# Decoder layer on one core: the feed-forward stage and the end go through the same instruction recorder as the stages before

## The chip, the cores and the metric

The kernel runs on one core of a Trainium2 chip. That core has five instruction streams: TensorE (PE) for matmuls, VectorE (DVE), ScalarE (ACT) and GpSimd (POOL) for elementwise work, and SyncE (SP), which here only issues DMA transfers. Each stream runs its instructions in the order in which the program has them; a semaphore wait holds up everything behind it in the same stream. The metric is the device time in microseconds (us) of one execution.

## The reference

One layer of a decoder is computed in float32 for a prompt of 512 tokens and for 8 samples of 4 tokens each, 544 token columns in all, with shared weights (1024 model channels, 2816 feed-forward channels):

```python
h = rmsnorm(x, norm_mix)
z = h @ w_in                       # dilated attention: q, k, v; HGRN2: q, f, i, gate
att = dilated_attention(...)       # three (window, dilation) patterns, 8 heads of 64
o, s_new = hgrn2_recurrence(...)   # 4 heads, 128 x 128 state, chunks
x = x + concatenate([att, o]) @ w_out
cq = rmsnorm(x, norm_cross) @ w_cq
co = softmax(cq @ mem_k.T * X_DH ** -0.5) @ mem_v     # 4 heads, 256 memory rows
x = x + co @ w_co
u = rmsnorm(x, norm_ffn)
ug = u @ w_gate
up = concatenate([conv_buf, ug])   # two earlier rows
conv = conv_b + sum(conv_w[j] * up[:, j:j + T] for j in range(3))
x = x + (silu(conv) * (u @ w_up)) @ w_down
y = rmsnorm(x, norm_final)
```

Outputs are y for prompt and samples, the new keys and values, the memory's keys and values, the HGRN2 states and the last two gate rows of the convolution.

## The kernel before

Activations lie transposed, channels on partitions and the 544 tokens along the free axis. Every float32 operand of a large product is split in two parts, `h` (a cast to the PE's reduced float format, on ACT) and `l` (the rest, a subtraction on DVE), and a product is made of three passes, `h*h`, `l*h` and `h*l`. The tokens are cut in two halves: columns 0 to 256 and 256 to 544 (`CUTS`), and for the last product 0 to 288 and 288 to 544 (`LAST_CUTS`). A product of one output tile (128 channels) and one half goes to one PSUM tile: tag `dense` with two buffers, tag `aux` with five.

**Two planners.** The stages up to the end of the cross attention are *told* to a recorder, the class `Tape`. Its engine objects (`_Engine`) do not issue; they record each instruction as a part of a `Step`, with the tiles it reads and writes. Steps told inside `tape.main()` keep the order in which they are told (the backbone of dense products); all others are side steps. `Tape.due` works back from the backbone to a due time (`begin`) for each step. `Tape.plan` then runs an event loop: on each engine, of the side steps that are ready and due within `LEAD` = 15 us, the one with the earliest due time goes next, if its buffers are free (`fits`). Side steps of PE go in bursts between main ones. A step may also be held by a gate: it isn't told to run before a certain main step (`AHEAD` counts how many main steps back that lies). All this runs in three rounds, and then the calls are issued in the order found.

The feed-forward stage has another planner, `Plan`, with `Job`s whose lengths are written by hand. A `Job` for PE keeps its place; the rest gets a due time from its users and an optional `lead` before which it isn't begun. An evacuation of PSUM has `within`, a due time counted from the end of its product. The end of the kernel is written out without a planner: `ffn_last`, `last_by_half` and `last_half` issue products, with lists `evacs` and `pending` that hold back the work on the results by one step, and `sides` pumps one generator step (`conv_last`, `final`) after each product.

**The feed-forward stage.** 22 gate tiles and 22 up tiles (`ug`, `up`) of 128 channels. Tiles 0 to 3 are plain: 24 matmuls for each half (`ps_g0_0`, `ps_g0_256`, `ps_u0_0` and so on). Tiles 4 to 21 go in pairs by a Strassen-Winograd scheme of seven products: 2 x 2 blocks over (channel tile, token half) and model channels. It needs sums of weight blocks (up to signs): `S1` of A21 and A22 and `S3` of A11 and A21, which come by a plain load through SP followed by an accumulating load through POOL's software queue (`load_sum`), and `S2` of S1 and A11 and `S4` of S2 and A12 on DVE, and sums of activation blocks `X, T, U, V` (`combine`), each split in `h` and `l` again. A name like `S1u10` is the sum S1 for the pair of up tiles 10 and 11. On the finished gate tile ACT, DVE and ACT make the convolution and silu (`cv`); POOL copies its last rows out (`last<-ug`), multiplies `up` by `cv` for the prompt (`up<-up,cv`), and ACT and DVE split the result to `h3h`, `h3l` and so on (one pair for each tile). Down products of four tiles at a time (`ps_d0_m` for tiles 0 to 3 and output tile m, then `d4`, `d8`, `d12`, `d16` for two tiles) stand between the pairs' products, and are added to the residual `xr` by DVE.

**The end.** The last four tiles (18 to 21) go down as `ps_dz`, first half for all eight output tiles, then the second half. Squares of the final residual are summed on POOL (`acc_final`), the column sums are made by PE (`psr_final`), ACT makes the reciprocal root by a logarithm and an exponential (`r_fin`), for which a table has to be loaded, and DVE and POOL scale the result (`y`). The first half's `final(0)` is pumped while the second half's products run.

Large SBUF tiles of one size share a tag `a` with 59 buffers. In `Tape.plan` such a tile is given out early only if 12 (`SPARE`) stay free, unless it is due within 8 us (`SOON`).

Of the kernel before, what the change touches and what calls it, by code (L numbers as in the profile page):

```python
# [16 lines left out]
D = 1024  # L17
# [153 lines left out]
class Job:  # L171


    def __init__(self, engine, length, fn, deps, lead=None, within=None, takes=None, gives=None):
        self.engine, self.length, self.fn, self.lead = engine, length, fn, lead
        self.within, self.takes, self.gives = within, takes, gives
        self.deps, self.users = [d for d in deps if d is not None], []
        for d in self.deps:
            d.users.append(self)


class Plan:

    STEP = 0.1

    def __init__(self, **banks):
        self.jobs, self.order, self.banks = [], [], {tag: [0.0] * n for tag, n in banks.items()}

    def add(self, engine, length, fn, *deps, **more):

        self.jobs.append(Job(engine, length, fn, deps, **more))
        return self.jobs[-1]

    def pe(self, length, fn, *deps, takes=None):
        self.order.append(self.add("PE", length, fn, *deps, takes=takes))
        return self.order[-1]

    def run(self):

        t = 0.0  # L200
        for i, j in enumerate(self.order):
            j.place, j.begin = i, t
            t += j.length
        late = t + 100.0
        for j in reversed(self.jobs):
            if j.engine != "PE":
                j.begin = min([u.begin for u in j.users] + [late]) - j.length - self.STEP
                if j.within is not None:
                    j.begin = min(j.begin, max(d.begin + d.length for d in j.deps if d.engine == "PE") + j.within)
        for i, j in enumerate(self.jobs):  # L210
            j.waits, j.number = len(j.deps), i
            j.ready = 0.0 if j.lead is None else max(0.0, j.begin - j.lead)
        free, done = {}, []
        waiting = [j for j in self.jobs if not j.waits]
        left, now, place = len(self.jobs), 0.0, 0
        while left:
            best, soonest = None, None
            for j in waiting:
                if j.engine == "PE" and j.place != place:
                    continue  # L220
                if j.takes and not self.banks[j.takes]:
                    continue
                start = max(j.ready, now, 0.0 if j.engine == "SP" else free.get(j.engine, 0.0),
                            min(self.banks[j.takes]) if j.takes else 0.0)
                soonest = start if soonest is None else min(soonest, start)
                if start <= now + 1e-9 and (best is None or (j.begin, j.number) < (best.begin, best.number)):
                    best = j
            if best is None:
                assert soonest is not None
                now = soonest  # L230
                continue
            waiting.remove(best)
            left -= 1
            best.start, best.end = now, now + best.length
            if best.engine == "PE":
                place += 1
            free[best.engine] = best.end
            if best.takes:
                self.banks[best.takes].remove(min(self.banks[best.takes]))
            if best.gives:  # L240
                self.banks[best.gives].append(best.end + self.STEP)
# [2011 lines left out]
```

## Time and profile before

| | us |
|---|---|
| median of 3 executions | 839.62 (839.14 to 839.94) |
| profiled execution | 839.75 |
| its span in the trace | 838.0 |
| PE busy | 821.8 (98%) |
| DVE busy | 590.5 (70%) |
| ACT busy | 396.4 (47%) |
| POOL busy | 180.1 (21%) |
| mean granted PE clock | 0.996 |

The span is counted from the first to the last instruction of the trace; 1.75 us of the execution lie around it. Stages by time: mixing (norm, projections, attention, HGRN2, `w_out`) to about 370, cross attention to about 452, plain feed-forward tiles to about 503, pairs of tiles and down products to about 804, the last product and the final norm to 838. In the windows view a row has the window, its length, then for each of PE, PE weight loads, DVE, ACT and POOL the busy time and the number of instructions, then the granted PE clock, the busy share of the DMA engines and GB/s. In the list of waits a row has the engine, the operation that waited, what ended the wait, and the us in total, the number of times and the longest. In the timeline a row has start and duration, and in brackets how long the engine was idle before it and what ended that. In the list of groups a row ends with the busy time, the mean ns of one, and the idle time before them. In the list of transfers the last number is the median time in us from issue to landing.

### The profile page before, as it was taken

The numbers are of one execution on the slowest core, as the hardware profiler recorded it, in microseconds if no ns is written. First come the engines' busy times: TensorE is split into PE (matmuls) and PEld (weight loads), VectorE is DVE, ScalarE is ACT, GpSimd is POOL, SyncE is SP. The second block draws the span as 40 slices with busy tenths as digits, with TensorE's granted clock in tenths as the row PEclk, the third lists the DMA queues.
The fourth block names the chain that finished last, engine by engine and source line by source line (L and its number), as shares of the span: only waits on it lengthen the run. The fifth ranks groups of instructions, "written<-read, shape, count | busy, mean of one in ns | idle before, by whom it ended". The sixth has DMA issues, their size and how long they took to land.

```text
span 838.0 us, 18847 instructions
## 1 busy us (share of the span) xinstructions
PE 821.8 (98%) x7594; PEld 767.3 (92%) x7594; DVE 590.5 (70%) x1233; ACT 396.4 (47%) x792; POOL 180.1 (21%) x261
## 2 busy tenths in 40 slices
PE   9999999999999999999999999999999999999996
PEld 8988888778889879998889999999999999999995
DVE  6684735865888986564556899878777776777764
ACT  7412424443545644343545456465454554544633
POOL 1140000210120220222233232324213222322113
PEclk9999999999999999999999999999999999999999
DMA  9566787866842635260621237656544654564403
GB/s 320 203 188 185 235 264 239 293 203 201 282 141 85 200 89 160 75 223 27 222 91 51 81 92 184 157 144 171 144 128 127 153 161 122 145 154 114 136 23 108
DMA packets 90760, 132.33 MB, mean 158 GB/s; under 512 B 6064, under 2 KB 60080, under 8 KB 90544
## 3 DMA queue, kind: packets, MB, share of 16 engines
q1 hardware_dynamic: 84480, 120.69, 44.8%
q0 software_dynamic: 5184, 9.44, 6.9%
q8 instruction: 60, 0.98, 0.5%
q10 hardware_dynamic: 1008, 0.99, 0.4%
q14 instruction: 28, 0.23, 0.1%
HBM read 123.03 MB, written 8.07 MB: 156 GB/s over the span
## 4 chain that ended last, share of the span: by engine, by line
PE 88%; DVE 6%; issue 2%; DMA 2%; ACT 1%; POOL 0%; SPq 0%; DVEq 0%; POOLq 0%; ACTq 0%
PE ps_d L797 12%; PE ps_ag L2039 6%; PE ps_au L2039 6%; PE ps_wo L593 6%; PE ps_co L593 3%; PE ps_cg L2039 3%; PE ps_k L593 3%; PE ps_q L593 3%; PE ps_cq L593 3%; PE ps_hv L593 3%; PE ps_cu L2039 3%; PE ps_g L797 2%; PE ps_hq L593 2%; PE ps_hf L593 2%; PE ps_hg L593 2%; PE ps_dz L797 2%
## 5 line engine op out<-in xcount | busy, mean ns | idle before, releaser
L593 ACT CAST wh<-wr 128x1024 fp32r<-128x1024 f32 (+1 forms) x61 | 53.3, 892 | 109.7 <-PE ps_q L593 20.0
L593 DVE TENSOR_TENSOR wl<-wr,wh 128x1024 fp32r<-128x1024 f32 (+1 forms) x61 | 65.4, 1080 | 9.7 <-ACT wh L593 9.3
L593 POOL TENSOR_TENSOR hG<-hG,hf 128x256 f32<-128x256 f32 (+1 forms) x28 | 25.8, 921 | 192.2 <-DVE hf L593 142.2
L1809 POOL TENSOR_TENSOR up<-up,cv 128x512 f32<-128x512 f32 x22 | 33.1, 1506 | 142.0 <-ACT up L2018 64.3
L1530 DVE TENSOR_TENSOR xr<-xr,ps_d 128x256 f32<-128x256 f32 x80 | 34.7, 434 | 14.0 <-PE ps_d L797 13.1
L1796 DVE SCALAR_TENSOR_TENSOR cv<-ug,vec,cv 128x560 f32<-128x560 f32 x44 | 35.2, 800 | 4.0 <-ACT cv L1787 3.0
L1791 POOL COPY last<-ug 128x2 f32<-128x2 f32 x22 | 9.5, 432 | 97.6 <-ACT ug L2018 79.6
L593 POOL TENSOR_TENSOR acc_cx<-acc_cx,sq_cx 128x256 f32<-128x256 f32 (+1 forms) x14 | 12.4, 890 | 66.5 <-ACT sq_cx L593 66.3
L1787 ACT ACTIVATE cv<-ug,vec 128x560 f32<-128x560 f32 x22 | 18.9, 858 | 16.4 <-DVE ug L2058 11.1
L593 ACT ACTIVATE P<-P,mx 128x128 f32<-128x128 f32 (+3 forms) x32 | 17.6, 551 | 6.1 <-DVE mx L593 6.1
L593 DVE TENSOR_TENSOR xr<-xr,ps_wo 128x256 f32<-128x256 f32 (+1 forms) x16 | 6.8, 436 | 19.2 <-PE ps_wo L593 19.2
L593 PE MATMUL ps_co<-coh,wh 128*128 128x256 f32 (+1 forms) x64 | 19.7, 308 | 0.3 <-ACT coh L593 0.3
L1800 ACT ACTIVATE cv<-cv 128x560 f32<-128x560 f32 x22 | 14.8, 673 | 10.9 <-DVE cv L1796 9.9
L593 PE MATMUL ps_co<-col,wh 128*128 128x256 f32 (+1 forms) x64 | 19.3, 301 | 0.1
L593 PE MATMUL ps_co<-coh,wl 128*128 128x256 f32 (+1 forms) x64 | 19.1, 298 | 0.0
L719 DVE TENSOR_TENSOR wl<-wr,wh 128x512 fp32r<-128x512 f32 (+1 forms) x15 | 14.0, 936 | 6.0 <-ACT wh L710 6.0
L710 ACT CAST wh<-wr 128x512 fp32r<-128x512 f32 (+1 forms) x15 | 12.0, 814 | 9.6 <-PE ps_g L797 4.5
L2052 ACT COPY keptrg<-ps_ag 128x272 f32<-128x272 f32 x9 | 3.5, 385 | 27.3 <-PE ps_ag L2039 27.3
L593 PE MATMUL psd<-st,qbd_win 128*32 128x224 f32 x256 | 16.1, 359 | 0.0
L593 POOL TENSOR_TENSOR acc_ux<-acc_ux,sq_ux 128x256 f32<-128x256 f32 (+1 forms) x14 | 11.2, 798 | 22.2 <-ACT sq_ux L593 21.9
L1985 DVE TENSOR_TENSOR wlu<-wru,whu 128x1024 fp32r<-128x1024 f32 x9 | 12.7, 1407 | 4.5 <-ACT whu L1979 4.5
L1985 DVE TENSOR_TENSOR wlg<-wrg,whg 128x1024 fp32r<-128x1024 f32 x9 | 11.0, 1222 | 6.5 <-ACT whg L1979 6.5
(2659 smaller groups left out, 3608.1 us busy)
## 6 DMA issues: line engine op xcount, KB each, us to landing
st<-in_kwT SPq DMA_DIRECT2D x32, 448.0 KB, 5.3
st<-in_vw SPq DMA_DIRECT2D x28, 512.0 KB, 5.8
wr<-in_w_in SPq DMA_DIRECT2D x25, 512.0 KB, 5.7
wd<-in_w_down SPq DMA_DIRECT2D x32, 256.0 KB, 3.0
wrg<-in_w_gate SPq DMA_DIRECT2D x9, 512.0 KB, 5.5
wru<-in_w_up SPq DMA_DIRECT2D x9, 512.0 KB, 6.1
st<-in_mkT SPq DMA_DIRECT2D x8, 512.0 KB, 4.8
wr<-in_w_out SPq DMA_DIRECT2D x8, 512.0 KB, 4.1
```

What stands on the lines that cost most here:

```text
L593: return tape.put(engine, lambda: call(*args, **kw), outs, ins, length, lag, size)
L710: nc.scalar.copy(hi[:, :k1 - k0, :], raw[:, k0:k1, :])
L719: nc.vector.tensor_tensor(lo[:, :n, :], raw[:, k0:k1, :], hi[:, :n, :].bitcast(F32), op=ALU.subtract)
L797: nc.tensor.matmul(ps[:, :n], a, b[:, n0:n0 + n], start=(first and at == 0 and j == 0), stop=(last and at == len(order) - 1 and j == 2))
L1530: nc.vector.tensor_tensor(x[m][:, n0:n0 + n], x[m][:, n0:n0 + n], ps[:, :n], op=ALU.add)
L1787: nc.scalar.activation(hid[j][:, :W], ugs[j][:, :W], AF.Identity, bias=V("conv_b", j), scale=V("conv_w0", j))
L1791: nc.gpsimd.tensor_copy(last2[:, j, 0:2], ugs[j][:, SEQ:SEQ + 2])
L1796: nc.vector.scalar_tensor_tensor(hid[j][:, :W], ugs[j][:, i:i + W], V(f"conv_w{i}", j), hid[j][:, :W], op0=ALU.mult, op1=ALU.add)
L1800: nc.scalar.activation(hid[j][:, :W], hid[j][:, :W], AF.Silu)
L1809: nc.gpsimd.tensor_tensor(up[:, :SEQ], up[:, :SEQ], c[:, :SEQ], op=ALU.mult)
L1985: nc.vector.tensor_tensor(lo, self.raw, self.hi.bitcast(F32), op=ALU.subtract)
L2039: nc.tensor.matmul(ps[:, :HT], l, r, start=first and k == 0 and i == 0, stop=k == 3 and i == 2, skip_group_check=True)
```

## The change

`Plan` is removed. Its jobs, now without lengths, are collected by a class `Later`, which tells them to the recorder: a product of PE as a main step, and every other job as soon as the products it depends on have been told. The feed-forward stage and the end are recorded on the same tape as the rest, and there is a single `tape.run()` at the end of the kernel. The hand-written `evacs`, `pending`, `ffn_last` and `conv_last` go. In the recorder itself:

- a due time counts a transfer with 2.3 us and its bytes (`takes`), where it counted 0.1 us for the issue;
- PSUM evacuations of the tag `aux` are due soon after their product, as those of `dense` were;
- the rule for large tiles (`SPARE`, `SOON`) is replaced by `leaves_room`, which follows through the planned takes and last uses whether room is left for what is due before;
- a job's `lead` is kept by its step;
- a burst of side steps on PE also begins when one of them is past its due time;
- the buffers for raw and split weights are given out in the order told.

The weights of the last product get tiles of their own (`wdz`, `wdhz`, `wdlz` instead of the numbers 61 to 68), `final(0)` is told as a main step after the third product of the second half, and the load of the table is joined to the logarithm.

The instructions are the same on every engine (PE 6493, DVE 1235, ACT 749, POOL 266, SP 338 in the program); only their order differs.

```diff
-class Plan:
...
+class Later:
+    def tell(self, job):
+        if job.told:
+            return
+        for d in job.deps:
+            self.tell(d)
+        job.told = True
+        if job.main:
+            with self.tape.main():
+                job.fn()
+        else:
+            with self.tape.early(job.lead):
+                job.fn()
+
     def run(self):
+        left = self.jobs
+        for job in self.order:
+            self.tell(job)
+            for j in left:
+                if not j.told and j.mains and all(d.told for d in j.mains):
+                    self.tell(j)
+            left = [j for j in left if not j.told]
+        for j in left:
+            self.tell(j)
...
+    def takes(self):
+        return (2.3 + self.bytes / 300e3 if self.bytes else self.length) + self.lag
...
-    BURST, PATIENCE, SLACK, SPARE, SOON, LEAD = 1.0, 4.0, 12.0, 12, 8.0, 15.0
+    BURST, PATIENCE, SLACK, LEAD = 1.0, 4.0, 12.0, 15.0
...
-            ready = max([d.soon + d.length + d.lag for d in s.deps] + [0.0])
+            ready = max([d.soon + d.takes() for d in s.deps] + [0.0])
...
-                s.begin = s.soon + self.SLACK
+                s.begin = s.soon + (self.SLACK if s.lead is None else 100.0)
                 if s.engine in ("DVE", "ACT") and any(d.main for d in s.deps) and any(
-                        self.kinds.get(n) == "dense" for n in s.tiles):
+                        self.kinds.get(n) in ("dense", "aux") for n in s.tiles):
                     s.begin = max(d.est + d.length for d in s.deps if d.main) + 1.0
...
-                    s.begin = min(s.begin, u.begin - s.length - s.lag)
+                    s.begin = min(s.begin, u.begin - s.takes())
...
-            spare = self.SPARE if s.begin > clock[0] + self.SOON else 0
-            return all(room[k] >= v + spare * (k == "a") for k, v in needs(s).items())
+            want = needs(s)
+            return all(room[k] >= v for k, v in want.items()) and ("a" not in want or leaves_room(s, want["a"]))
+
+        def leaves_room(s, n):
+            have = room["a"] - n
+            ups = [(t, 1) for t in ends.values() if t < s.begin]
+            for name, t in takes:
+                if t >= s.begin:
+                    break
+                if name not in held and name not in s.tiles:
+                    ups.append((t, -1))
+                    if last[name] < s.begin:
+                        ups.append((last[name], 1))
+            for _, d in sorted(ups):
+                have += d
+                if have < 0:
+                    return False
+            return True
...
-                    can = [s for s in waiting[e] if s.ready <= now + 1e-9 and s.begin <= at and fits(s)]
+                    can = [s for s in waiting[e] if s.ready <= now + 1e-9 and s.begin <= at + (s.lead or self.LEAD) and fits(s)]
...
                 if side and (burst or not main or sum(s.length for s in side) >= self.BURST
-                             or now - first > self.PATIENCE):
+                             or now - first > self.PATIENCE
+                             or min(s.begin for s in side) < clock[0] + now - clock[1]):
...
     dense_by_half(co_hl, KT, "co", co_evac, co_after)
     r_ffn, ux = ffn_in.r, ffn_in.hl
+    tape.AHEAD = {"SP": 24, "ACT": 14, "DVE": 14, "POOL": 14, "PE": 14}
     ws.advance()
-    tape.run()
...
-        return job("SP", 5.0, lambda: None, job("POOL", 1.2, accumulate, load, lead=4.0)), box
+        return job(lambda: None, job(accumulate, load, lead=4.0)), box
...
-            done.append(job("DVE", out_cost(kind, n0), evac, p, rows_done if n0 else None, within=1.0,
-                            gives="dense"))
+            done.append(job(evac, p))
...
+        with tape.together():
+            if not c:
+                nc.scalar.preload_act_table_set(LN_SET)
+            nc.scalar.activation(r_fin[:, cut], ps[:, :n], AF.Ln, bias=eps, scale=1.0 / D)
...
+    held = []
+    for m in range(KT):
+        t, hi, lo = (A(f"{n}z{m}", [128, k, 128], dt) for n, dt in (("wd", F32), ("wdh", F32R), ("wdl", F32R)))
+        nc.sync.dma_start(t, w_down[m][:, 128 * DOWN_LAST[0]:128 * DOWN_LAST[1]].rearrange("p (k c) -> p k c", c=128))
+        nc.scalar.copy(hi, t)
+        nc.vector.tensor_tensor(lo, t, hi.bitcast(F32), op=ALU.subtract)
+        held.append([(hi[:, i, :], lo[:, i, :]) for i in range(k)])
+        last_half(m, 0)
+    for m in range(KT):
+        last_half(m, 1)
+        if m == 2:
+            with tape.main():
+                final(0)
+    with tape.main():
+        final(1)
+    tape.run()
```

More of the change, by code (lines that the diff above doesn't have):

```diff
@@ L192, in add, with __init__, pe @@
+class Later:
+    def __init__(self, tape):
+        self.tape, self.jobs, self.order = tape, [], []
+    def add(self, fn, *deps, lead=None):
+        self.jobs.append(Job(fn, deps, False, lead))
         return self.jobs[-1]
-    def pe(self, length, fn, *deps, takes=None):
-        self.order.append(self.add("PE", length, fn, *deps, takes=takes))
+    def pe(self, fn, *deps):
+        self.order.append(Job(fn, deps, True, None))
         return self.order[-1]
-    def run(self):
[L200 to L241, printed above, removed]
-            done.append(best)
-            for u in best.users:
-                u.ready = max(u.ready, best.end + self.STEP)
-                u.waits -= 1
-                if not u.waits:
-                    waiting.append(u)
-        for j in done:
-            j.fn()
-        return done
@@ L471, in start @@
                 room[k] -= v
+            for n in s.tiles:
+                if n in last and n not in held:
+                    ends[n] = last[n]
             held.update(n for n in s.tiles if n in self.kinds)
```

243 lines of the change are left out of this document (96 added, 147 removed).

## The prediction

> **What bounds the kernel now.** I read the page's engine totals and its chain first, then the table of windows by stage, then the list of what TensorE (PE) waited for, and only then single places.
>
> ```profile
> PE 821.8 (98%) x7594; PEld 767.3 (92%) x7594; DVE 590.5 (70%) x1233; ACT 396.4 (47%) x792; POOL 180.1 (21%) x261
> PE 88%; DVE 6%; issue 2%; DMA 2%; ACT 1%; POOL 0%; SPq 0%; DVEq 0%; POOLq 0%; ACTq 0%
> ```
> ```profile
> 400.00:450.00 50.00, 49.63 (x407) 43.05 (x407) 29.75 (x69) 24.46 (x71) 15.24 (x20) 0.97 0.42 137
> 500.00:600.00 100.00, 98.94 (x789) 98.73 (x788) 83.85 (x143) 56.22 (x104) 30.93 (x51) 1.00 0.60 156
> 600.00:700.00 100.00, 100.00 (x800) 100.00 (x799) 74.32 (x131) 50.16 (x93) 26.55 (x44) 1.00 0.53 142
> 700.00:800.00 100.00, 99.67 (x791) 99.05 (x790) 75.39 (x141) 49.48 (x96) 22.57 (x36) 1.00 0.52 138
> 800.00:838.00 38.00, 29.88 (x227) 28.60 (x225) 20.25 (x41) 14.43 (x31) 12.02 (x15) 0.95 0.18 60
> sum 838.00, PE 821.79 PEld 767.28 DVE 590.51 ACT 396.43 POOL 180.10; mean PE 74.71 PEld 69.75 DVE 53.68 ACT 36.04 POOL 16.37
> ```
> PE is busy for 821.8 of 838.0 us. The change removes no instruction: the two programs hold the same ones on every engine, so PE's own work stays, and only the 16.2 us in which it is idle, and the stretches with a low clock, can be won. In the feed-forward stage (450 to 800) there is next to nothing: 600:700 is full. The 8.1 us missing in 800:838 are mostly the last reduction and the stores.
>
> ```profile
> PE ps_cp L593 <- DVE cq L593: 1.5, 1, 1.5
> PE ps_d L797 <- DVE h3l L1820: 1.1, 1, 1.1
> PE ps_cv L593 <- DVE mk L593: 0.7, 1, 0.7
> PE psdo L593 <- DMA st<-in_vw: 0.5, 1, 0.5
> PE ps_u L797 <- DVE ug L1888: 0.5, 1, 0.5
> PE psu L593 <- ACT hsm L593: 0.5, 1, 0.5
> ```
> Every named wait is single and short. The change must be costed as a handful of places that it moves, some for the better, some for the worse.
>
> **The change part by part.** The order that the recorder now writes was compared with the old one, engine by engine.
>
> *Cross attention, the sample's matmuls.* The 16 small ps_cos matmuls came after the last co block of the first half, with only their own dependants behind them. Now they stand between two co blocks (co4 and co5 of the first half), so three blocks hide coh.
>
> ```profile
> 435.22 1.85 PE L593 MATMUL ps_cos<-cs,com 128*128 128x16 f32 x16
> 437.35 0.40 PE L593 MATMUL ps_co<-coh,wh 128*128 128x288 f32 x1 [0.28 <-ACT coh L593]
> ```
> ```profile
> 438.00:440.00 2.00, 2.00 (x10) 2.00 (x11) 0.08 (x1) 0.58 (x2) 1.47 (x2) 0.55 0.35 98
> 440.00:442.00 2.00, 2.00 (x12) 2.00 (x11) 1.19 (x3) 0.87 (x2) 0.00 (x0) 0.60 0.00 0
> ```
> The wait of 0.28 goes: -0.3. Right behind it the granted clock is 0.55 and 0.60 in two windows of 2 us, which cost 2 x 0.45 + 2 x 0.40 = 1.7 us. The row does not say why; what stands before it is 1.85 us of thin matmuls and the gap. In the new order thin matmuls are followed at once by full ones. I take -1.7; the other bound is 0, if thin matmuls alone suffice. The Trainium skill (TensorE: Matmul & The Clock Gate, What's actually happening) says that the clock halves after an idle window of about 3.4 us, and that the window runs freely. By it a gap of 0.28 us should not have lowered the clock at all; the trace disagrees, or the thin matmuls counted as idle, and by the strict reading this term would be 0.
>
> *Cross attention, the queries.* The sum psr_cx of the first half stood after ps_cq1 and PE then waited for cq; now psr_cx comes before ps_cq1's 24 matmuls.
>
> ```profile
> 373.33 0.28 PE L593 MATMUL ps_cq<-cx0h,wh 128*128 128x256 f32 x1
> 376.14 0.60 PE L593 MATMUL psr_cx<-acc_cx,cs 128*128 128x256 f32 x2
> 378.21 1.78 PE L593 MATMUL ps_cp<-mk,cq 128*128 128x256 f32 x7 [1.47 <-DVE cq L593]
> ```
> Those 24 take 376.14 - 373.33 = 2.8 us, longer than the wait of 1.47. I take -1.2, bounds -1.5 and 0 (if the accumulated squares are not ready 2.8 us earlier).
>
> *First plain tiles.* The wait of ps_u for ug (0.5) came from an evacuation that stood late in VectorE's (DVE's) queue. PSUM evacuations of both kinds now fall due 1 us after their matmuls: -0.5, the other bound 0.
>
> *The rest of the mixing stage.* Streams, weight loads and heads are reordered. The waits there (mk 0.7, st 0.5, hsm 0.5 and smaller ones) could go, or double. I take 0, bounds -1.7 and +2.5.
>
> *Start of the paired tiles.* Here POOL changes for the worse. The accumulating load of S1g4 was issued ahead of the two copies last<-ug3; now it stands behind them, and S3g4 stands behind the product of tile 3.
>
> ```profile
> 499.99 0.71 POOL L1792 COPY last<-ug 128x16 f32<-128x16 f32 x1
> 504.25 1.61 POOL L1809 TENSOR_TENSOR up<-up,cv 128x512 f32<-128x512 f32 x1 [2.01 <-DVE up L1888]
> 506.00 0.65 ACT L1817 CAST h3h<-up 128x544 fp32r<-128x544 f32 x1 [0.58 <-DVE up L1813]
> 507.45 0.71 DVE L1820 TENSOR_TENSOR h3l<-up,h3h 128x544 fp32r<-128x544 f32 x1
> ```
> ```profile
> 511.64 0.29 PE L2039 MATMUL ps_cg<-Xh,S3g4h 128*128 128x272 f32 x1
> ```
> ```profile
> S1g<-in_w_gate POOLq DMA_DIRECT2D x9, 256.0 KB, 5.0
> S1u<-in_w_up POOLq DMA_DIRECT2D x9, 256.0 KB, 4.6
> S3u<-in_w_up POOLq DMA_DIRECT2D x9, 256.0 KB, 6.7
> ```
> ```profile
> 605.70 0.68 DVE L2029 TENSOR_TENSOR S2u<-S1u,wru 128x512 f32<-128x512 f32 x1
> ```
> S1g4 goes out at 499.99 + 0.71 = 500.7 and lands 5.0 later, at 505.7. DVE, which is in order, then does S2g4 (0.68, by the row of S2u) and V_0 (another 0.68), to 507.1; ScalarE (ACT) casts Vh_0 and then h3h (0.65 each), to 508.4; h3l takes 0.71, to 509.1. It ended at 507.45 + 0.71 = 508.2, and PE already waited for it. That is +0.9; with a landing of 4.6 it is +0.5, with 6.7 +2.6. I take +0.7. S3g4, issued at 505.9 behind the product, is needed near 511.6: with 4.6 to 5.0 and its cast and split (0.65, 0.71) just in time, with 6.7 about 1.6 late; alone in its queue it is nearer to the first, 0.
>
> *Steady paired tiles.* The load of S1u10 now stands behind the product of tile 9.
>
> ```profile
> 604.05 1.67 POOL L1809 TENSOR_TENSOR up<-up,cv 128x512 f32<-128x512 f32 x1 [3.12 <-DVE up L2058]
> 613.77 0.29 PE L2039 MATMUL ps_au<-Uh,S2u10h 128*128 128x272 f32 x1
> ```
> 605.7 + 4.6 + 0.68 + 0.65 + 0.71 = 612.4, 1.4 us before PE's need. So 0; it decides only where a landing takes over 6.0 us, and at 6.7 each unit would lose 0.7. The planner now counts such a load at 2.3 us, 0.9 for its bytes and a lag; the rows say 4.6 to 6.7. The Trainium skill (DMA: Bandwidth & Descriptors, Anatomy of one DMA) fits about 2.0 us + bytes / 436e3 for a load through this queue, 2.6 us here by estimate; by that the start above would cost nothing, and the sum would be -2.6. The accumulating loads of this trace need twice that, so the rows decide.
>
> *Last down tiles.* Weight splits for the last product move ahead, among the evacuations of the group before.
>
> ```profile
> 788.00:796.00 8.00, 7.67 (x61) 7.47 (x60) 6.92 (x16) 5.18 (x12) 2.58 (x2) 1.00 0.55 167
> 796.00:804.00 8.00, 8.00 (x60) 7.50 (x59) 6.18 (x15) 0.68 (x2) 0.00 (x0) 1.00 0.18 58
> L719 DVE TENSOR_TENSOR wl<-wr,wh 128x512 fp32r<-128x512 f32 x6 | 4.1, 686 | 0.0
> ```
> ```profile
> L1796 DVE SCALAR_TENSOR_TENSOR cv<-ug,vec,cv 128x560 f32<-128x560 f32 x44 | 35.2, 800 | 4.0 <-ACT cv L1787 3.0
> ```
> DVE had 13.1 us of rows in 16.0. It gets six more splits (4.1) and, late, a tap of tile 21 (two of 0.8, I count one): 18.0. Rows overlap a little at their ends (507.45 starts before the row ahead of it is over), so the true load is nearer to 15 or 16. Bounds 0 and +2.0; I take +0.7.
>
> *The end.* The sum psr_final of the first half moves behind dz2 of the second, and the table load from a free place to right before the logarithm.
>
> ```profile
> 817.19 1.28 ACT L2171 ACT_TABLE_LOAD   x1
> 820.05 0.50 ACT L2147 ACTIVATE r_fin<-psr_final,eps 128x288 f32<-128x288 f32 x1 [1.14 <-PE psr_final L2146]
> 820.58 0.44 ACT L2153 ACTIVATE r_fin<-r_fin 128x288 f32<-128x288 f32 x1
> 827.12 0.75 POOL L855 TENSOR_TENSOR acc_final<-acc_final,sq_final 128x256 f32<-128x256 f32 x1 [0.33 <-ACT sq_final L854]
> ```
> r_fin was there at 820.58 + 0.44 = 821.0. Now dz2's 12 matmuls come first (1.4 us at the pace of ps_cq's 24 in 2.8), which with its evacuation and square brings ACT to about 821.4, and then 1.28 + 0.50 + 0.44 follow with the load uncovered: 823.6. POOL then has three products and three sums of about 0.7 each before the last sum is done: 823.6 + 4.3 = 827.9, where it ended at 827.12 + 0.75 = 827.9. No room is left for anything late: bounds 0 and +1.0, taken +0.4.
>
> **The sum.** -1.7 - 0.3 - 1.2 - 0.5 + 0.7 + 0.7 + 0.4 = -1.9. The profiled execution took 839.75 us (span 838.0 and 1.75 around it), 0.13 above the median of 839.62. So 837.85 for its like, 837.7 for the median. A measurement of this kernel can tell about 0.2%, 1.7 us.
>
> **The rivals.** *The clock falls elsewhere.* The thin matmuls are still there, and if they lower the clock by themselves the 1.7 is paid again: -0.2, 839.4. For it speaks that the gap was so short; against it, that the feed-forward windows, with full matmuls alone, keep 1.00. The same result comes if the costs at the start of the pairs and at the end reach their upper bounds, or if the new order does in effect what the old one did (then 839.6). Together 0.30.
>
> *Late accumulating loads (slower).* If landings take 6.7 us in the new places, the start loses 2.6 and 1.6 instead of 0.7, and six u units (10 to 20) lose 0.7 each: -1.9 + 3.5 + 4.2 = +5.8, 845.4; with a few of the units +3, 842.6. It decides from 6.0 us on. Against it: S1u's median of 4.6, and that its neighbour S3u is now issued over 2 us later, which leaves it the queue. 0.18.
>
> *Weight loads in the mixing stage come later than their products (slower).* With +2.5 there and the clock term lost too, since a waiting PE is what may lower it: -1.9 + 2.5 + 1.7 = +2.3, 841.9. It decides where a load lands more than its present margin late; no row of before shows such a wait but the 0.5 of psdo for st. 0.10.
>
> **How the numbers follow.** The forecast (faster, 837.7, its own range 835 to 838) has 0.42. The second case makes 0.30 for the same, the last two 0.28 for slower. The low end, 834.5, is the sum with the costs near 0 and part of the mixing waits gone (-1.7 - 0.3 - 1.5 - 0.5 - 1.1 = -5.1); the high end, 843.5, holds the late loads in a few units.
>
> **What would show it.** After the change: no window below 0.9 around the ps_cos matmuls; no wait of ps_cp for cq above 0.3; h3l ending about 0.9 later relative to the first down block; S2u10l done over 1 us before its matmul; waits of ps_d for xr near the last down tiles up to 1 us; r_fin about 2.6 us later relative to the end of dz7 of the first half. It is wrong if PE waits for S2 or S3 splits in unit after unit, if a low clock appears at another place, or if the windows up to 400 lose more than 2 us of PE time.

## The result and the profile after

| | before | after |
|---|---|---|
| median of 6 executions on the same chip, us | 839.69 (839.0 to 840.42) | 842.85 (841.47 to 845.1) |
| profiled execution, us | 839.75 | 841.47 |
| its span, us | 838.0 | 839.7 |
| its mean granted PE clock | 0.996 | 0.998 |

The ratio is 1.004, 95% interval 1.0025 to 1.0056: slower by 3.2 us, where 2.0 us faster was forecast. The profiled execution of after is the fastest of its six, so its trace shows 1.7 us of the 3.2. The rest has to be found in what executions differ in. One execution of the kernel before on another chip, of 3759 us, is left out of all numbers below.

The page of after first (its line of engine totals), then its windows by stage with two narrow windows behind the small `ps_cos` matmuls (which start at 430.8 to 432.4 here) and two around the last down tiles, then the waits of PE (engine, operation, what ended the wait; us in total, times, longest).

```profile
PE 821.3 (98%) x7594; PEld 765.3 (91%) x7594; DVE 592.0 (70%) x1233; ACT 395.3 (47%) x792; POOL 182.9 (22%) x261
```
```profile
400.00:450.00 50.00, 50.00 (x423) 43.17 (x421) 30.38 (x69) 25.27 (x70) 15.91 (x19) 1.00 0.43 136
500.00:600.00 100.00, 98.72 (x785) 98.32 (x784) 77.61 (x134) 52.24 (x100) 27.72 (x43) 1.00 0.58 148
600.00:700.00 100.00, 100.00 (x799) 100.00 (x798) 75.52 (x131) 49.63 (x94) 25.84 (x42) 1.00 0.55 143
700.00:800.00 100.00, 98.02 (x775) 97.19 (x774) 74.20 (x140) 51.22 (x100) 25.88 (x41) 1.00 0.52 140
800.00:839.70 39.70, 30.94 (x227) 28.80 (x225) 18.90 (x40) 12.38 (x27) 11.93 (x15) 0.97 0.17 57
...
434.00:436.00 2.00, 2.00 (x19) 2.00 (x18) 1.28 (x4) 0.82 (x2) 1.10 (x2) 1.00 0.97 304
436.00:438.00 2.00, 2.00 (x18) 2.00 (x17) 0.91 (x3) 1.30 (x4) 1.11 (x2) 1.00 0.09 31
...
788.00:796.00 8.00, 7.50 (x57) 6.88 (x55) 7.22 (x17) 6.39 (x15) 1.47 (x3) 1.00 0.12 41
796.00:804.00 8.00, 6.52 (x42) 5.58 (x42) 8.00 (x17) 1.79 (x3) 1.44 (x1) 1.00 0.00 0
```
```profile
PE ps_d L606 <- DVE xr L606: 1.5, 2, 1.1
PE ps_dz L606 <- DVE xr L606: 1.4, 1, 1.4
PE psA L606 <- issue: 1.4, 1, 1.4
PE ps_u L606 <- DVE ug L606: 1.2, 1, 1.2
...
PE ps_d L606 <- ACT h3h L606: 0.7, 1, 0.7
...
PE ps_d L606 <- DVE h3l L606: 0.6, 1, 0.6
```
PE does the same work in the same busy time. The wait of `ps_cp` for `cq` and that for `coh` are gone, 400:450 is full, and the windows behind `ps_cos` stand at 1.00 where before they had 0.55 and 0.60. Against that stand new waits: for `xr` in two places, for `h3h`, and one of 1.2 for `ug` at 484.9. That is another `ug` than the one PE waited 0.5 for in before, at 474.6; the old wait is gone. The window 796:804 shows the largest: DVE is busy for 8.00 of 8.00 us, and PE falls from 8.00 to 6.52.

A ledger shows how this adds up. It compares the start of the same PE instruction in the two traces; each line gives by how much the lead changes within the stretch.

| stretch, up to the start of | after minus before, us |
|---|---|
| first `ps_cq` (mixing stage and `w_out`) | +0.8 |
| first `ps_cp` (the wait for `cq`) | -1.15 |
| second half of co block 3 (`coh`, clock) | -2.1 |
| first down product (plain tiles, `ug`) | -0.1 |
| its second half (`h3h`, `h3l`) | +0.5 |
| block 4 of the last down group (steady pairs) | +0.4 |
| first `ps_dz` (rest of that group) | +2.35 |
| last `psr_final` (the end) | +1.65 |
| end of the span | -0.6 |
| sum (the lines are rounded) | +1.7 |

Both large losses are seen in DVE's queue. The timeline of after has start, duration, engine, operation, and in brackets the idle time before and what ended it:

```profile
798.75 0.44 DVE L606 TENSOR_TENSOR xr<-xr,ps_d 128x288 f32<-128x288 f32 x1
799.12 0.68 DVE L606 TENSOR_TENSOR wdlz<-wdz,wdhz 128x512 fp32r<-128x512 f32 x1
799.25 0.40 PE L606 MATMUL ps_d<-h16h,wd_5h 128*128 128x288 f32 x1 [1.14 <-DVE xr L606]
799.72 0.41 DVE L606 TENSOR_TENSOR xr<-xr,ps_d 128x256 f32<-128x256 f32 x1
800.05 0.68 DVE L606 TENSOR_TENSOR wdlz<-wdz,wdhz 128x512 fp32r<-128x512 f32 x1
...
824.00 0.44 ACT L606 ACTIVATE r_fin<-r_fin 128x288 f32<-128x288 f32 x1
824.48 3.05 DVE L606 SCALAR_TENSOR_TENSOR y<-xr,vec,r_fin 128x288 f32<-128x288 f32 x3 [0.39 <-ACT r_fin L606]
827.45 0.41 DVE L606 TENSOR_TENSOR xr<-xr,ps_dz 128x256 f32<-128x256 f32 x1
827.78 0.93 DVE L606 SCALAR_TENSOR_TENSOR y<-xr,vec,r_fin 128x288 f32<-128x288 f32 x2
827.91 0.39 PE L606 MATMUL ps_dz<-h18h,wdhz 128*128 128x256 f32 x1 [1.44 <-DVE xr L606]
828.45 0.86 POOL L606 TENSOR_TENSOR acc_final<-acc_final,sq_final 128x256 f32<-128x256 f32 x1 [1.24 <-ACT sq_final L606]
```
A `wdlz` split, wanted only at 804, goes between two evacuations, each of which gives a PSUM buffer back to PE. At the end three scaled outputs stand ahead of an evacuation, and with two `dense` buffers PE waits for it.

### The profile page after: what moved, and what is told of

Same layout as the page of the kernel before. It is cut to its first block, busy times and chain, and to the rows that moved or that the text cites. A ratio compares the mean times of both kernels' runs of the same rounds, so it can differ in the third digit from the quotient of the medians.

```text
span 839.7 us, 18801 instructions
## 1 busy us (share of the span) xinstructions
PE 821.3 (98%) x7594; PEld 765.3 (91%) x7594; DVE 592.0 (70%) x1233; ACT 395.3 (47%) x792; POOL 182.9 (22%) x261
## 4 chain that ended last, share of the span: by engine, by line
PE 84%; DVE 10%; issue 2%; DMA 1%; ACT 1%; POOL 1%; SPq 0%; DVEq 0%; POOLq 0%
PE ps_d L606 12%; PE ps_au L606 6%; PE ps_ag L606 6%; PE ps_wo L606 6%; PE ps_cg L606 3%; PE ps_cu L606 3%; PE ps_co L606 3%; PE ps_k L606 3%; PE ps_cq L606 3%; PE ps_hf L606 2%; PE ps_hq L606 2%; PE ps_v L606 2%; PE ps_hv L606 2%; PE ps_hg L606 2%; PE ps_dz L606 2%; PE ps_first L606 2%
## 5 line engine op out<-in xcount | busy, mean ns | idle before, releaser
L606 ACT CAST wh<-wr 128x1024 fp32r<-128x1024 f32 (+1 forms) x68 | 60.9, 908 | 109.3 <-PE ps_k L606 16.9
L606 DVE TENSOR_TENSOR wl<-wr,wh 128x1024 fp32r<-128x1024 f32 (+1 forms) x68 | 72.4, 1073 | 11.8 <-ACT wh L606 11.6
L606 DVE SCALAR_TENSOR_TENSOR cv<-ug,vec,cv 128x560 f32<-128x560 f32 x44 | 38.2, 868 | 0.2
L606 POOL COPY last<-ug 128x2 f32<-128x2 f32 (+1 forms) x44 | 19.9, 481 | 77.6 <-ACT ug L606 49.5
L606 DVE TENSOR_TENSOR xr<-xr,ps_dz 128x288 f32<-128x288 f32 (+1 forms) x16 | 7.0, 436 | 13.3 <-PE ps_dz L606 13.3
L606 ACT COPY keptru<-ps_au 128x272 f32<-128x272 f32 x9 | 3.5, 386 | 25.1 <-PE ps_au L606 25.1
L606 PE MATMUL psdo<-st,dpt 128*32 128x256 f32 x224 | 15.2, 385 | 0.0
L606 DVE TENSOR_TENSOR hf<-hf 128x256 f32<-128x256 f32 (+1 forms) x28 | 11.9, 425 | 4.7 <-POOL hG L606 4.4
```

What stands on the lines that cost most here:

```text
L606: return tape.put(engine, lambda: call(*args, **kw), outs, ins, length, lag, size)
```

## The experiments

The theory after the first look: the two queue places in DVE cost 1.8 and 1.5 us, the start of the pairs another 0.5 and, since PE stands still there, sometimes a low clock. The rivals: the late exponential is what costs at the end; landings of the accumulating loads cost in every unit; the mixing stage, or the new rules of the recorder as such, are worse. Ratios are to the kernel before on the same chip.

**The changed kernel again, unaltered.** It asks what differs between executions.

> The changed kernel once more, unaltered. Its six executions so far lie between 841.5 and 845.1 us while the kernel before stays within 839.0 to 840.4, and the profiled one, with a span of 839.7, was the fastest. Theory 1 (some executions get a lower TensorE clock at a wait that the new order made longer): the longer executions have the lower mean granted clock (0.994 to 0.996 against 0.998), and a profile that is longer than 839.7 shows a window of about 3.4 us at a clock near 0.5 behind one of the waits of 1 us or more (ps_d or ps_dz for xr near the end, or psA near 227). Rival (the spread comes from DMA landings in the mixing stage): the clock is the same and a wait for a DMA differs by 1 us or more.

841.4 us (840.27 to 844.18), ratio 1.0033, interval 1.0019 to 1.0047. From its list of waits:

```profile
PE ps_d L606 <- ACT h3h L606: 1.5, 1, 1.5
...
PE psA L606 <- issue: 0.8, 1, 0.8
```
The wait for `h3h` was 0.7 in the first trace and is 1.5 here; the one of `psA` was 1.4 and is 0.8. Four of ten executions had a mean clock of 0.997 or less. The three at 0.996 are the three slowest (843.03 to 844.18), as theory 1 had it, but the window with the low clock itself is in no profile of this kernel; and the six at 0.998 still differ by 2 us. So two or three quantities vary, and one profile doesn't stand for the median.

**The recorder's rules alone.** The kernel before with the classes `Step` and `Tape` of after; the feed-forward stage and the end stay with `Plan` and the handwritten order. Run twice, on two chips.

```diff
-    BURST, PATIENCE, SLACK, SPARE, SOON, LEAD = 1.0, 4.0, 12.0, 12, 8.0, 15.0
+    BURST, PATIENCE, SLACK, LEAD = 1.0, 4.0, 12.0, 15.0
...
+    def takes(self):
+        return (2.3 + self.bytes / 300e3 if self.bytes else self.length) + self.lag
...
```


> The kernel before, with the new rules of the recorder for the stages up to the end of cross attention; the feed-forward stage and the end are ordered by the old planner and by hand. Theory 1 (the new rules gained what the prediction said, 1.5 for cq and 2 for coh and the clock, less about 1 in the mixing stage; what was lost lies in the feed-forward stage and the end): 837 us, faster than before by 2 to 3. Rival (the mixing stage costs as much as cross attention gains, and the profiled execution was a lucky one): 839.5 to 841, with the same wide spread as the changed kernel.

837.74 us, ratio 0.999 (0.9977 to 1.0004). In its order `ps_cos` still comes last of its half, with the wait for `coh` behind it, and yet its profile has no low clock there:

```profile
436.00:438.00 2.00, 1.63 (x12) 1.32 (x12) 0.57 (x5) 1.06 (x6) 0.00 (x0) 1.00 0.03 6
438.00:440.00 2.00, 2.00 (x17) 2.00 (x16) 0.77 (x2) 0.17 (x2) 0.73 (x1) 1.00 0.34 89
```
Its lead of 1.5 to 1.7 us over the trace of before is as large as the missing dip (0.8 lost in the mixing stage and some 0.8 won at the queries cancel); it is kept through the feed-forward stage to the end. Whether the order had anything to do with it needed the second run.

> The new rules for the stages before the feed-forward stage with the old order behind them, once more beside the other. Theory 1: a span near 836, clock 0.998 in most executions. Rival (its low number of executions with a low clock was luck, since the thin matmuls and the wait for coh stand as before): a clock of 0.996 or less in half of the executions, and a median 1 us higher.

838.83 us, ratio 1.0001 (0.9991 to 1.001), and 8 of 11 executions at 0.996 or less, where it had been 2 of 12. The dip is there again. The windows below are cut at the change of the clock, of this kernel first, of before second:

```profile
434.87:438.28 3.41, 3.07 (x26) 2.76 (x24) 1.07 (x6) 1.52 (x7) 0.73 (x1) 1.00 0.02 5
438.28:441.69 3.41, 3.38 (x14) 3.38 (x15) 1.00 (x5) 0.46 (x2) 0.73 (x1) 0.50 0.21 55
```
```profile
434.78:438.19 3.41, 3.04 (x25) 2.73 (x24) 1.30 (x6) 1.27 (x8) 0.18 (x2) 1.00 0.04 7
438.19:441.60 3.41, 3.41 (x17) 3.41 (x16) 0.85 (x2) 0.90 (x4) 1.29 (x2) 0.50 0.18 53
```
So the rules by themselves are worth nothing that can be measured (the theory was 2 to 3 us), and the dip at this place comes and goes with one and the same order of instructions. The 0.3 to 0.4% of the change come from the feed-forward stage and the end.

**The end undone.** On after: the table load joined to the last square of the first half, `final(0)` after the second product.

```diff
-            nc.scalar.activation(last_sq[:, cut], x[m][:, cut], AF.Square)
+            with tape.together():
+                nc.scalar.activation(last_sq[:, cut], x[m][:, cut], AF.Square)
+                if not c:
+                    nc.scalar.preload_act_table_set(LN_SET)
...
-        if m == 2:
+        if m == 1:
```


> The changed kernel, with the end as it was: the table is loaded right behind the last square of the first half, and the sum of the first half goes to TensorE ahead of the third product of the second half. Theory 1 (the exponential comes 3 us late, three scaled outputs then stand ahead of the evacuation of xr4 on VectorE, and TensorE waits 1.4 us for a bank, then everything behind is late): 2.0 to 2.4 us faster than the changed kernel, about 840.5, and no wait of ps_dz for xr. Rival (the end is set by GpSimd's chain of sums, which has as much to do as before): 0.5 or less.

842.29 us, ratio 1.0037 (1.0023 to 1.0052). `r_fin` is there at 821.6 instead of 824.4, and in the trace it helps by 0.1 us from the first `ps_dz` to the last `psr_final`: PE's wait for `xr` is 1.3 instead of 1.4. The median shows no gain either (the changed kernel had 841.4 on this chip). DVE's timeline shows why:

```profile
821.63 1.16 DVE L606 SCALAR_TENSOR_TENSOR y<-xr,vec,r_fin 128x288 f32<-128x288 f32 x1 [1.75 <-ACT r_fin L606]
822.72 0.41 DVE L606 TENSOR_TENSOR xr<-xr,ps_dz 128x256 f32<-128x256 f32 x1
823.05 2.69 DVE L606 SCALAR_TENSOR_TENSOR y<-xr,vec,r_fin 128x288 f32<-128x288 f32 x3
825.66 0.41 DVE L606 TENSOR_TENSOR xr<-xr,ps_dz 128x256 f32<-128x256 f32 x1
```
One output goes first; the run of three comes 1.4 us earlier and again stands ahead of an evacuation. So the late exponential alone is not the cause. That the run of outputs is one is tested two experiments further on.

**The end, and the splits held back.** On the kernel above: the split of `wdlz` from the third on may not be placed earlier than two main steps before the place where it is told.

```diff
+        tape.gate_at = len(tape.mains) - 2 if m > 1 else None
+        tape.cut()
         nc.vector.tensor_tensor(lo, t, hi.bitcast(F32), op=ALU.subtract)
+        tape.cut()
+        tape.gate_at = None
```


> As t1_end_undone, and the splits on VectorE of the last product's weights from the third on are held back until the last product runs, two output tiles ahead of their use, as before the change. Theory 1 (those splits stood among the evacuations of the d16 group and cost 1.2 us net): 1.0 to 1.5 faster than t1_end_undone, about 839.2. Rival (the group is held by the late cast of wd16_6 and by tile 21, not by the splits): within 0.4 of t1_end_undone.

839.82 us, ratio 1.0008 (0.9997 to 1.0018). The last down group:

```profile
788.00:796.00 8.00, 7.44 (x60) 7.24 (x59) 7.22 (x17) 6.96 (x15) 1.30 (x1) 1.00 0.14 48
796.00:804.00 8.00, 7.61 (x55) 6.95 (x55) 6.64 (x16) 2.66 (x5) 1.67 (x1) 1.00 0.01 2
...
503.85:507.26 3.41, 1.74 (x13) 1.35 (x12) 3.41 (x7) 2.94 (x7) 1.74 (x2) 1.00 0.89 189
507.26:510.67 3.41, 3.41 (x17) 3.41 (x16) 3.41 (x7) 2.38 (x4) 0.00 (x0) 0.50 1.00 237
```
In 796:804 DVE drops from 8.00 to 6.64 and PE gets 1.1 us back; from block 4 to the first `ps_dz` the loss against before is 0.55 instead of 2.35. Holding back the splits is worth 1.8 us there (the medians of the two kernels differ by 2.5; 1.0 to 1.5 were expected). The late cast that the rival names shows in after as a wait of 0.5 for `wd_6h` at 793.3, in block 3, ahead of this stretch, so it is no part of the 2.35. The lower two rows are news: a low clock after the waits for `h3h` and `h3l`, as long as the one that the change had removed at `ps_cos`.

**The outputs spread.** On that: the scaled outputs of the first half are told in pairs, each behind one of the products `dz3` to `dz6` of the second half (counted from 0).

```diff
-        for m in range(KT):
+        if c:
+            scaled(c, r, range(KT))
...
+        if 2 < m < 7:
+            tape.gate_at = len(tape.mains) - 1
+            tape.cut()
+            scaled(0, r_fin[:, slice(*LAST_CUTS[0])], range(2 * m - 6, 2 * m - 4))
...
```


> As td_end_and_splits, and the eight scaled outputs of the first half are told in pairs behind the third to the seventh product of the second half, so that VectorE has at most two of them ahead of an evacuation. Theory 1 (TensorE's wait of 1.3 us at dz5 comes from three or four scaled outputs standing ahead of the evacuation of xr3 or xr4, whatever the time of the exponential, which is why the earlier exponential alone won nothing): the wait of ps_dz for xr is under 0.3 us, and the median is 1.2 to 1.6 us below td_end_and_splits. Rival (the last sum on GpSimd sets the end in any case): no change within 0.4, with the wait moved to psr_final.

839.7 us, ratio 1.0005 (0.9996 to 1.0015); median span 837.2, where the kernel above had 838.05 and the kernel before 837.2 and 837.3 beside the two. In the trace PE no longer waits for `xr` in the last product, and the stretch from the second half of `ps_dz` to the last `psr_final` takes 1.5 us less (13.98 instead of 15.50; before 14.01):

```profile
822.28 0.41 DVE L606 TENSOR_TENSOR xr<-xr,ps_dz 128x256 f32<-128x256 f32 x1
822.61 0.73 DVE L606 SCALAR_TENSOR_TENSOR y<-xr,vec,r_fin 128x288 f32<-128x288 f32 x1
823.26 0.41 DVE L606 TENSOR_TENSOR xr<-xr,ps_dz 128x256 f32<-128x256 f32 x1
823.60 0.74 DVE L606 SCALAR_TENSOR_TENSOR y<-xr,vec,r_fin 128x288 f32<-128x288 f32 x1
824.47 0.42 DVE L606 TENSOR_TENSOR xr<-xr,ps_dz 128x256 f32<-128x256 f32 x1
```
So the run of outputs is what cost at the end, with the exponential early; spreading the outputs with the late exponential was not run. The 1.2 to 1.6 us expected for the median did not come: set against the kernel before beside each, the median span fell by 0.75 and the ratio from 1.0008 to 1.0005. The time outside the span hides part of it: it has a median of 2.3 us here (1.7 to 3.0), and of 1.9 for the kernel before beside it. Why is open. The profile has the low clock at the start of the pairs again:

```profile
503.42:506.83 3.41, 1.72 (x12) 1.39 (x11) 3.41 (x7) 2.75 (x6) 1.71 (x2) 1.00 0.77 168
506.83:510.24 3.41, 3.41 (x17) 3.41 (x16) 3.41 (x7) 2.47 (x4) 0.00 (x0) 0.50 0.97 244
```

**Due times that know the real landing.** If the planner's 2.3 us for an accumulating load is the fault, 5.3 should help. Once on the kernel above, once on after.

```diff
-        return (2.3 + self.bytes / 300e3 if self.bytes else self.length) + self.lag
+        return (2.3 + 3.0 * (self.engine == "POOL") + self.bytes / 300e3 if self.bytes else self.length) + self.lag
```


> As t2_outputs_spread, and the recorder's due times count an accumulating load on GpSimd's queue with 3.0 us more (5.3 us and its bytes instead of 2.3), in the due times alone. S1g4 is then issued ahead of the copies of tile 3's last rows, S3g4 ahead of the product of tile 3, and S1u10 ahead of the product of tile 9. Theory 1 (VectorE waits 0.7 to 1.1 us for S1g4 ahead of h3l, and TensorE then waits 0.7 to 1.5 for h3h and 0.6 for h3l): VectorE no longer waits for that load, the two waits sum to 1.1 or less as before the change, 0.5 to 1.0 faster than t2_outputs_spread, and fewer executions with a clock of 0.995 or less. Rival (VectorE and ScalarE are busy there anyway and h3 is as late): within 0.3.

> The changed kernel with the due times of accumulating loads alone corrected (3.0 us more), the end and the splits as in the changed kernel. Theory 1: 0.5 to 1.0 faster than the changed kernel's 841.4 to 842.9, so 840.5 to 842. Rival that I named in the prediction (late loads cost 0.7 in unit after unit, and are the main loss): 4 us or more faster.

On the kernel above: 842.34 us, ratio 1.0036 (1.0023 to 1.0049), against 1.0005 without it. On after: 845.7 us, ratio 1.0077 (1.0061 to 1.0094), the slowest of all. The wait for `h3h` is 2.5 and 3.0 us. ACT's timeline, of the second:

```profile
505.68 0.62 ACT L606 CAST S3g4h<-S3g 128x512 fp32r<-128x512 f32 x1 [3.33 <-DMA S3g<-in_w_gate]
506.20 0.64 ACT L606 CAST Vh<-V 128x544 fp32r<-128x544 f32 x1
506.75 0.64 ACT L606 CAST h3h<-up 128x544 fp32r<-128x544 f32 x1
```
The load of `S3g4` was indeed issued earlier (497.78 instead of 502.57). But the edit changes the due times alone. The recorder's event loop still lets a transfer land 2.0 us and its bytes after its start (0.9 for 256 KB, and a lag of 0.3; more if others are under way), so with the earlier load it also placed the cast of `S3g4` earlier in ACT's queue, ahead of `h3h`. The landing took 7.9 us, and ACT stood for 3.33 with `h3h` behind it. Moving the load moved its user as well. The steady pairs show that nothing was to be won there: from the second half of the first down product to the first product of the last down group this kernel is 0.3 us behind before, and so is after.

**The first two loads early.** On the kernel with the outputs spread: the accumulating loads of `S1g4` and `S3g4` alone get due times 9 us earlier, without a new estimate of their length; no due time of a user is set.

```diff
+            if s.lead == 12.0:
+                s.begin -= 9.0
...
-        return job(lambda: None, job(accumulate, load, lead=4.0)), box
+        return job(lambda: None, job(accumulate, load, lead=12.0 if name in ("S1g4", "S3g4") else 4.0)), box
```


> As t2_outputs_spread, and the due times of two accumulating loads, S1g4 and S3g4, are set 9 us earlier (and their lead to 12 us), no others. S1g4 is then issued ahead of the product of tile 2, in a stretch where GpSimd only waited, S3g4 right behind that product, and ScalarE casts h3h ahead of S3g4 and of Vh. The correction of all such loads by 3 us made it worse (h3h waited 2.5 to 3.0), since S1g4 still stood behind the product of tile 2 and ScalarE had the cast of S3g4 ahead of h3h. Theory 1 (one load behind one late product, in an in-order queue, is what costs): VectorE does not wait for S1g, TensorE's waits for h3h and h3l sum to 1.2 or less instead of 1.7, the profiled span without a low clock is 0.5 to 0.9 below t2's 836.2 to 836.5, and the clock falls in fewer executions (2 of 12 or less below 0.997). Rival (V_0, V_1 and the order of VectorE hold h3l in any case): the sum of the two waits stays above 1.5.

836.74 us (836.01 to 839.1), ratio 0.998, interval 0.9971 to 0.999: 0.2% faster than the kernel before, and faster than the changed one. From its waits:

```profile
PE psA L608 <- issue: 1.4, 1, 1.4
...
PE ps_d L608 <- DVE h3l L608: 1.0, 1, 1.0
```
The wait for `h3h` is gone, `h3l` is as before (1.1). Here too the users moved: ACT casts `h3h` at 503.02, ahead of `S3g4h` (503.58, without a wait) and of both `Vh`, where after had a `Vh` ahead of `h3h`, and `S3g4h` behind them all. Nine of twelve executions have a mean clock of 0.998 or more, and its profile shows no low clock anywhere between the first products and the last reduction.

## Why the prediction was wrong

Two terms for VectorE's queue failed. The last down tiles were taken at +0.7 and cost 2.35, and the end was taken at +0.4, by GpSimd's chain, and cost 1.65 by a run of outputs on VectorE. Beside them a low clock that comes in about half of the executions was counted as a fixed gain of 1.7.

**Clock and `coh`: right in the trace, wrong as a price.** Forecast -1.7 and -0.3, measured -2.1. But I took a dip that one profile showed for a fixed cost of the order of instructions. Of 66 executions of before, on three chips, 30 had a mean clock of 0.996 or less and 22 one of 0.998; one dip is 3.41 x 0.5 / 838 = 0.002. The spans at 0.996 have medians of 837.5 to 837.7, those at 0.998 of 836.0 to 836.8. If the executions at 0.996 or less are those with the dip (its one trace has the dip), it is paid in about half of them, and its removal is worth about 0.8 us by estimate, not 1.7.

**The rival that the clock falls elsewhere: its condition came true.** It was priced as "the gain is lost". What happened: the new waits at the start of the pairs leave PE idle for 1.3 to 2.1 us (3.0 and more with the altered due times), and a dip appears there in four of the seven profiles with this start, those of the splits held back, of the outputs spread and of the two with altered due times. Both profiles of after are free of it, but not all of its executions are: five of its sixteen have a mean clock of 0.996 or less. That is part of why the median (+3.2) lies above the trace (+1.7): of the first six, the three at 0.998 have spans of 839.7 to 840.8, the other three of 841.4 to 843.3. That these five fell at the same spot is inferred from the other kernels, whose order up to there is the same; no trace of after shows it.

**The queries: right.** -1.15 for -1.2, and no wait of `ps_cp` for `cq`.

**`ug`: right about the wait, but another came.** Forecast -0.5. The wait of 0.5 (474.6 in before) is gone, and one of 1.2 stands 10 us later (484.9), so the plain tiles come out at -0.1. The new one is not in every execution: the second profile of after lacks it, and there the plain tiles come out at -1.0. In the first profile a small product on DVE ahead of that evacuation (`up<-up,cv`, 32 columns, 482.40) takes 1.32 us beside POOL's product of 1.67; in the second it takes 0.17, and POOL's takes 2.37.

**Start of the pairs: right in mechanism.** `S1g4` landed 4.7 us after its issue (5.0 was taken); S2, V, `h3h` and `h3l` followed in the order described, `h3l` 0.5 later against the first down product (0.9 forecast), +0.5 us (+0.7; the second profile has +1.3). Not seen was that the wait splits into two, for `h3h` and then for `h3l`, with a single matmul between them. PE stands idle for 1.3 us in all here, for 2.1 in the second execution, and that is where the clock can fall.

**Steady pairs: right.** No unit waits for a load; `S2u10l` ends at 610.3 and its matmul starts at 612.1. The rival of late loads in every unit is out: 600:700 is full. The drift of +0.4 over 290 us belongs to no single wait (the part with the wait for `wd_6h` comes out at +0.1).

**Last down tiles: the term that failed most.** +0.7 was taken, +2.35 measured, just above the upper bound of 2.0. The mechanism was named, the size was taken from a sum of DVE's load over 16 us. The sum says whether the queue is full, not who stands behind whom: a 0.68 split ahead of a 0.44 evacuation can delay PE by up to its whole length when the other of the two `dense` buffers is full too, and DVE had no free time from 791 to 804. Holding the splits back brought 1.8 of the 2.35 back; the other 0.55 is open. A full queue should have pointed to the upper bound.

**The end: right about `r_fin`, wrong about who waits.** `r_fin` came 2.65 us later against the first half's end (2.6 forecast), but the chain that I followed, POOL's products and sums, was idle: before its next sum POOL waits 1.24 us for ACT, and ACT for `xr`. What cost was DVE's run of outputs ahead of an evacuation: +1.65 for the +0.4 taken, outside its bound of 1.0; spreading the outputs brought 1.5 of it back. The -0.6 behind the last `psr_final` is no gain of the order: the kernel with the new rules alone, whose end is that of before, also needs 7.3 us from there instead of 7.9.

**The mixing stage: 0 taken, +0.8 measured, inside its bounds.** It varies between executions of one order (the second profile of after has -0.3), and in the nine other profiles of changed kernels `ps_wo` begins between 0.3 earlier and 1.45 later than in before. A part of it is PE's wait of `psA` for its own instruction stream ("issue"), 0.7 to 1.5 us. Where that comes from is open.

By terms the miss in the trace is 3.6 us: last down tiles 1.65, mixing 0.8, the end 0.6 net, `ug` and plain tiles 0.4, steady drift 0.4, less 0.2 at the start of the pairs. The other 1.4 us of the miss lie between the profiled execution and the median. Clock, mixing and the start of the pairs are seen to vary; what share each has is open.

## What to carry to other kernels

For a queue that is served in order, ask of each instruction moved ahead of a PSUM evacuation when its result is wanted; a sum of the load over a stretch finds the full queue but not the price. When a planner moves a load, it moves the load's user too, and an earlier load can make things worse if the user then blocks a queue for a landing that takes 4 to 10 us in these traces: after such a change, look at the queue in which the user stands. Before a low clock in one profile is put into a sum, look at the mean clock of all the executions.

## What the runs showed of the hardware

**The clock goes by windows of fixed length.** In all eleven traces the changes of the granted clock lie on a grid of 3.41 us. Its offset is the same within a trace and another one in each execution. Away from the two ends of a run there are six dips. Five are one such window at 0.50, which costs 1.7 us; the sixth, in the kernel with the outputs spread and altered due times, is two windows, 6.83 us. A dip follows a window in which PE streamed little, not only one in which it was idle. Counted from the matmul records after 380, a full window has 26 to 29 matmuls of 256 columns and more; the windows ahead of the six dips had 6 (before, and 16 thin ones), 7 (the new rules again, and 16 thin ones), 10 (splits held back), 10 (outputs spread), 5 and 1 (the two with altered due times), and no window with 13 or more was followed by one. That is no sharp bound: near the end of a run, windows with 9 (after, from 830.2) and 8 (outputs spread with altered due times, from 830.6) were not followed by one. In the window 434.78:438.19 above PE is busy for 3.04 of 3.41 us and yet a dip follows; sixteen of its matmuls are only 16 columns wide. In the first run of the rules alone the same matmuls and the same gap fell astride two windows, the poorer of which had 14 wide ones, and no dip came. That fits one order having it in a part of its executions; three traces of this place (two with a dip, one without) are all that shows it. The Trainium skill (TensorE: Matmul & The Clock Gate, What's actually happening) gives a free-running window of 3413 ns, which agrees. It asks for an idle window before the clock falls; here a window with 10 of 27 wide matmuls was enough, and the measurement decides.

**VectorE is slower beside a busy GpSimd, in some places.** Three outputs on DVE take 1.02 us each (824.48) while POOL multiplies its own two and adds a square, and 0.47 each at 827.78, when POOL mostly doesn't: 1.65 us more in a place where PE waits for the evacuation behind them. Beside the rows shown above stand these, of after:

```profile
824.52 1.79 POOL L606 TENSOR_TENSOR y<-y,r_fin 128x288 f32<-128x288 f32 x2 [1.48 <-ACT r_fin L606]
826.28 0.93 POOL L606 TENSOR_TENSOR acc_final<-acc_final,sq_final 128x256 f32<-128x256 f32 x1
...
833.73 2.44 DVE L606 SCALAR_TENSOR_TENSOR y<-xr,vec,r_final 128x256 f32<-128x256 f32 x6 [2.17 <-ACT r_final L606]
```
The last row is the second half, whose factor `r_final` lies in PSUM and not in SBUF: there six outputs take 0.41 us each, though POOL multiplies two of its own beside them from 834.23 on, for 1.41 us. So not every output on DVE is slower beside POOL; that the place of the factor decides was not tested. In the changed kernel with altered due times (the second of the two) two V sums at the start of the pairs take 2.46 us while POOL multiplies, and 1.35 in after, where it doesn't. That POOL's products are the cause was not tested by moving them.
